# Three of eleven gate and up pairs of a gated FFN by seven block products, and the down product in two passes

## The chip, the cores and the metric

The kernel runs on one core of a Trainium2 chip. Its engines are TensorE (PE, with its weight load shown apart as PEld), VectorE (DVE), ScalarE (ACT), GpSimd (POOL) and SyncE (SP, which here only issues DMAs). The metric is the device time of one execution in microseconds; of several runs the median is given.

## The reference

One encoder block on 256 tokens of width 2048, all in float32. A mixer (a Hyena branch and a Conformer branch, gated and merged) comes first; behind it stands the channel part, which the change touches:

```python
h = rms_norm(x, ffn_pre_g[l])
gu = h @ ffn_w_gu[l]                               # 2048 x 11264
gate, up = gu[..., :FFN_HIDDEN], gu[..., FFN_HIDDEN:]   # FFN_HIDDEN = 5632
x = x + rms_norm((jax.nn.silu(gate) * up) @ ffn_w_down[l], ffn_post_g[l])
```

## The kernel before, in words

**Float32 in three products.** TensorE multiplies in a rounded float32 form (`F32R`), so each operand is split into a rounded part `hi` and the rest `lo`, and each product is hi·hi + lo·hi + hi·lo: three matmuls. For a weight tile of 128 partitions by 1024 elements (512 KB) the split is a cast on ScalarE (L299) and a subtraction on VectorE (L300), both in `split_raw`. The weight tile comes by a DMA from SyncE's queue into one of four `raw` buffers; `hi` and `lo` have three buffers each, so a tile's cast waits until TensorE has read the `hi` of the tile three before it.

**Gate and up.** `chunk_as` (L355) makes 512 columns of the result for all 256 tokens: eight groups, each of one weight tile (two contraction blocks of 128), and per group 2 blocks x 2 token halves x 3 = 12 matmuls of 128x128 by 128x512, 96 in a chunk. The activations are the stationary operand: `h2T`, eight tiles of 4 KB per partition, already split. The eleven pairs (a gate chunk, then an up chunk, L1133 to L1140) take two of the four PSUM banks called `main` per chunk. Then `silu` (ScalarE, L1116) and `glu` (VectorE, L817) turn a pair into 512 columns of the gated result; `glu` goes on to transpose it (eight transposes on TensorE, L1126, into the PSUM banks called `aux`), and splits it into two tiles of `hid` (a cast on ScalarE, L1128, and a subtraction on VectorE, L1129). All 22 `hid` tiles are there before the down product begins.

**Down.** `product_as` (L382) multiplies the 44 contraction blocks of `hid` with `w_down`. All 2048 columns and both token halves are summed at once, in four `aux` and four `main` banks. Each of the 88 weight tiles (one block, 1024 columns) feeds 12 matmuls. The last four blocks are held back, split into spare tiles, and run result by result (token half t, 512 columns n, 12 matmuls each), so that each of the eight results can be finished while the next runs. `done` in `post_norm` (L966) squares a result on ScalarE (L272), multiplies it by the gain on VectorE (`gained`), and at the last result of a token half makes the norm's factor (`late_rstd`) and calls `finish_block` (L1142), which adds the residual in five pieces on VectorE (L1148) and writes each out (L1151).

**Memory and order.** Everything that isn't a `raw`, `hi` or `lo` buffer, or one of eight 2 KB `t5` tiles, lies in one pool, `big`, of 35 slots of 4 KB per partition: `h2T` 8, `hid` 22, the residual 4, the gated results one each. Work that follows a chunk is written as a generator that yields estimated costs; `pump(budget)` after each group of matmuls steps the generators in the queue, which sets the program order. A list scheduler then orders each engine's instructions by that program order and by its own simulated times, and each engine runs its list strictly in order.

## Time and profile before

| | us |
|---|---|
| median of 3 runs (lowest, highest) | 1399.36 (1397.22, 1399.64) |
| the profiled execution, its own time | 1399.35 |
| its span, first to last instruction | 1397.5 |
| TensorE busy in the span | 1384.8 |
| VectorE busy | 867.2 |
| ScalarE busy | 669.2 |

The mean granted clock of TensorE was 0.997 of full speed. The busy time of TensorE is that of matmuls that overlap each other (one lasts 391 ns and the next begins 227 ns after it), so it hides gaps shorter than a matmul; the chain of waits, which counts the steps from one instruction to the next, is the finer measure. The time outside the span is 1.85 us.

### The profile page before, as it was taken

To read this page: it belongs to the slowest core of one execution; us is meant where nothing else is said; L and a number is where in the kernel's file an instruction comes from. 1 tells how busy PE (TensorE), PEld (TensorE's weight loads), DVE (VectorE), ACT (ScalarE), POOL (GpSimd) and SP (SyncE) were. 2 spreads that over 40 slices of the span, in tenths; PEclk is the share of its full clock that TensorE was granted. 3 is DMA by queue.
4 is the path that set the end of the run, shared out by engine and by line. 5 is a ranking of instruction groups with operands and counts; after the bars stand their busy time and mean duration, and the time that the engine had idled before them with its cause. 6 is when DMAs were issued, how large, how long until landed. Compare 5 with 4: busy or idle time off the path is not lost.

```text
span 1397.5 us, 16896 instructions
## 1 busy us (share of the span) xinstructions
PE 1384.8 (99%) x6438; PEld 1153.3 (83%) x6438; DVE 867.2 (62%) x1084; ACT 669.2 (48%) x844; POOL 11.9 (1%) x23
## 2 busy tenths in 40 slices
PE   9999999999999999999999999999999999999997
PEld 8888888888888878888888888888888888888885
DVE  6888777778777777547754544545455544444445
ACT  6556555455565444446744444444444444333343
POOL 0000000000000000000000000000000000000000
PEclk9999999999999999999999999999999999999999
DMA  9676555554454655755566666666666665656653
GB/s 343 214 218 200 152 184 178 166 166 151 150 190 145 185 161 160 274 191 183 182 194 184 194 192 186 193 185 193 190 187 190 187 220 190 193 195 194 197 185 132
DMA packets 76544, 264.58 MB, mean 189 GB/s; under 512 B 8689, under 2 KB 10002, under 8 KB 76464
## 3 DMA queue, kind: packets, MB, share of 16 engines
q1 hardware_dynamic: 75520, 261.74, 59.5%
q0 software_dynamic: 944, 1.77, 0.4%
q8 instruction: 50, 0.82, 0.2%
q14 instruction: 30, 0.25, 0.1%
HBM read 261.38 MB, written 2.10 MB: 189 GB/s over the span
## 4 chain that ended last, share of the span: by engine, by line
PE 98%; DVE 1%; DMA 0%; ACT 0%; SPq 0%; issue 0%; DVEq 0%; ACTq 0%
PE main L87 80%; PE aux L87 16%; PE aux L1126 1%; DMA raw<-in_w_in_dram 0%; PE aux L705 0%; PE aux L941 0%; PE aux L621 0%; PE aux L1020 0%; PE aux L578 0%; DVE big L1148 0%; DVE lo L300 0%; ACT t L272 0%; ACT hi L299 0%; SPq L156 0%; DVE t L201 0%
## 5 line engine op out<-in xcount | busy, mean ns | idle before, releaser
L300 DVE TENSOR_TENSOR lo<-raw,hi 128x1024 fp32r<-128x1024 f32 x447 | 546.2, 1223 | 435.5 <-ACT hi L299 408.8
L299 ACT CAST hi<-raw 128x1024 fp32r<-128x1024 f32 x447 | 470.7, 1054 | 634.2 <-PE main L87 593.2
L87 PE MATMUL main<-hi,big 128*128 128x512 f32 x2824 | 717.5, 391 | 1.8 <-ACT big L201 1.2
L87 PEld LDWEIGHTS main<-hi,big 128*128 128x128 f32 x2824 | 528.5, 188 | 112.3 <-ACT big L201 1.7
L87 PE MATMUL main<-lo,big 128*128 128x512 f32 x1412 | 392.0, 390 | 0.0
L87 PEld LDWEIGHTS main<-lo,big 128*128 128x128 f32 x1412 | 265.1, 188 | 55.3 <-issue 0.2
L87 PE MATMUL aux<-hi,big 128*128 128x512 f32 x416 | 111.7, 389 | 0.0
L87 PE MATMUL main<-big,hi 128*128 128x512 f32 (+1 forms) x448 | 97.8, 363 | 0.7 <-ACT hi L217 0.5
L87 PEld LDWEIGHTS aux<-hi,big 128*128 128x128 f32 x416 | 77.9, 188 | 16.1
L87 PEld LDWEIGHTS main<-big,hi 128*128 128x128 f32 x448 | 73.9, 190 | 13.4 <-ACT hi L217 1.5
L87 PE MATMUL aux<-big,big 128*128 128x512 f32 x288 | 76.5, 391 | 0.0
L87 PE MATMUL aux<-lo,big 128*128 128x512 f32 x208 | 64.3, 389 | 0.0
L87 PEld LDWEIGHTS aux<-big,big 128*128 128x128 f32 x288 | 53.7, 188 | 11.6 <-DVE big L300 0.4
L87 PEld LDWEIGHTS main<-big,lo 128*128 128x128 f32 x384 | 51.7, 191 | 3.1
L87 PE MATMUL main<-big,lo 128*128 128x256 f32 x384 | 53.2, 282 | 0.0
L87 PEld LDWEIGHTS aux<-lo,big 128*128 128x128 f32 x208 | 39.0, 188 | 8.1
L87 PE MATMUL main<-big,big 128*128 128x512 f32 x132 | 31.9, 393 | 0.0
L300 DVE TENSOR_TENSOR big<-raw,big 128x1024 fp32r<-128x1024 f32 x16 | 19.6, 1226 | 14.6 <-ACT big L299 14.5
L87 PEld LDWEIGHTS main<-big,big 128*128 128x128 f32 x132 | 24.4, 188 | 4.9
L299 ACT CAST big<-raw 128x1024 fp32r<-128x1024 f32 x16 | 16.8, 1053 | 18.1 <-DMA raw<-in_w_down_dram 9.5
L817 DVE SCALAR_TENSOR_TENSOR big<-main,rstd,big 128x512 f32<-128x512 f32 x22 | 15.5, 747 | 12.0 <-PE main L87 12.0
L663 ACT CAST big<-t 128x512 fp32r<-128x512 f32 x24 | 14.7, 618 | 6.4 <-DVE t L662 6.3
(212 smaller groups left out, 627.0 us busy)
## 6 DMA issues: line engine op xcount, KB each, us to landing
raw<-in_w_gu_dram SPq DMA_DIRECT2D x176, 512.0 KB
raw<-in_w_as_dram SPq DMA_DIRECT2D x96, 512.0 KB
raw<-in_w_down_dram SPq DMA_DIRECT2D x88, 512.0 KB
raw<-in_w_in_dram SPq DMA_DIRECT2D x44, 512.0 KB
raw<-in_w_out_dram SPq DMA_DIRECT2D x32, 512.0 KB
raw<-in_hy_proj_dram SPq DMA_DIRECT2D x16, 512.0 KB
raw<-in_cf_proj_dram SPq DMA_DIRECT2D x16, 512.0 KB
raw<-in_w_in_dram SPq DMA_DIRECT2D x8, 256.0 KB
```

The costliest lines, as they stand in the source:

```text
L87: return nc.tensor.matmul(o, lhsT, rhs, start=start, stop=stop, skip_group_check=True)
L299: S.copy(hi[:, k], raw[:, k])
L300: V.tensor_tensor(out=lo[:, k], in0=raw[:, k], in1=hi[:, k], op=ALU.subtract)
L663: nc.scalar.copy(rs[j][ft][:, 0], v)
L817: nc.vector.scalar_tensor_tensor(out=d[:, t], in0=ps[t], scalar=scale[t], in1=d[:, t], op0=ALU.mult, op1=ALU.mult)
L1126: nc.tensor.transpose(tr[:, c, t * P:(t + 1) * P], sg[:, t, f:f + P], ident)
```

## The change

Pairs 1, 2 and 3 of the eleven no longer go through `chunk_as`. The generator `seven` treats one pair as a product of 2 by 2 blocks: the tokens' two halves by the two halves of the 16 contraction blocks (`k`), times these halves by gate and up. It forms seven products of sums and differences of such blocks in place of eight products of blocks (Strassen's scheme in Winograd's form). The four sums of tokens are made once (`sums_of_tokens`) and split into eight slots; the four differences of weights are made for each pair on VectorE (`less`), from tiles that are loaded into `big` slots, and are then split as any weight tile. A pair takes twelve steps: in part one, four steps of two products (p1, p5); in part two, four of three (p3, p7, p6); in part three, four of two (p2, p4). A product has six matmuls in a step. Behind parts one, two and three the products are added up (`first_out`, `second_out`, `last_out`). After every second group of the other pairs' chunks, `tick` takes one step.

No result is turned into `hid` when it is made: the gated results stay as they are, one slot each, and `make_hid` transposes and splits each of them during the first pass of the down product. That product, `product_halves`, goes over all 44 blocks for the first 1024 columns and then again for the others, in four banks a pass; the results of the first pass are finished during the second, and the last four blocks of the second pass are held back.

```diff
+SEVENS = 3
...
     def chunk_as(w, act, budget):
...
             pump(budget)
+            tick()
         return ps
...
+    def product_halves(w, nkt, act, budget, late, done):
+        finished = deque()
+        for hf in range(2):
+            ps = [[(aux() if hf else psm.tile([P, 512], F32, tag="main", name=nm("main")))
+                   for _ in range(2)] for _ in range(2)]
+            held = []
+            for kt in range(nkt):
+                if not hf and kt % 4 == 0:
+                    hid = act(kt // 4)
+                ahead = hf and kt >= nkt - late
+                hi, lo = split_group(
...
+                if ahead:
+                    held.append((kt, hi, lo))
+                    continue
...
+                pump(budget)
+                if hf and kt and finished:
+                    done(*finished.popleft())
+            if not hf:
+                finished.extend((t, j, ps[t][j]) for t in range(2) for j in range(2))
...
+    def make_hid(c):
+        def begin(c):
+            if len(hid) == 2 * c and c < len(gated):
+                hid.extend(slot([P, 2, 2, T], F32R) for _ in range(2))
+                turning.append(push(to_hid(gated[c], hid[-2:]), front=not c))
+        begin(c)
+        drain(list(turning))
...
+        begin(c + 1)
+        return hid
...
+    def sums_of_tokens():
+        for m in range(4):
+            f, r = slot([P, 2, 2, T]), slot([P, 4, 2, P])
+            sh, sl = slot([P, 4, 2, P], F32R), slot([P, 4, 2, P], F32R)
...
+    def seven(i, v):
+        def load(q, m):
+            r = slot([P, 2, 512])
+            nc.sync.dma_start(r, a["w_st"][i, q, m])
+            return r
...
+        def product(o, of, m, parts):
+            hi, lo = parts
+            for j in range(2):
+                for n, (s, w) in enumerate(((0, hi), (1, hi), (0, lo))):
+                    mm(o, of(m, j, s), w[:, j, :], (m, j, n) == (0, 0, 0), (m, j, n) == (3, 1, 2))
...
+        def second_out(p6, p3, p7, u5, u1, u3, c12):
+            add(u3, p6, u1)
+            add(c12, u3, u5)
+            yield 1.4
+            add(c12, p3, c12)
+            add(u3, p7, u3)
+            yield 1.4
+            add(u5, u3, u5)
+            yield 0.7
...
+        for m in range(4):
+            b11, b12 = load(0, m), load(1, m)
+            w1 = split_raw(b11)
+            tt.append(slot([P, 2, 512]))
+            less(tt[m], b12, b11)
+            wt = split_raw(tt[m])
+            product(p1, token(0, 0), m, w1)
+            product(p5, total(1), m, wt)
+            yield
+        out = emptied(first_out(p5, p1, u5, u1))
+        for m in range(4):
+            b22, b12 = load(3, m), load(1, m)
+            w3 = split_raw(b22)
+            if m == 0:
+                drain(out)
+                p6, p3, p7 = aux(), aux(), aux()
+            product(p3, total(4), m, w3)
+            less(b12, b22, b12)
+            product(p7, total(3), m, split_raw(b12))
+            less(tt[m], b22, tt[m])
+            product(p6, total(2), m, split_raw(tt[m]))
+            yield
+        out = emptied(second_out(p6, p3, p7, u5, u1, u3, c12))
+        for m in range(4):
+            b21 = load(2, m)
...
+            product(p2, token(1, 0), m, split_raw(b21))
+            less(tt[m], b21, tt[m])
+            product(p4, token(1, 1), m, split_raw(tt[m]))
+            yield
+        ends.extend(emptied(last_out(p4, p2, u5, u1, u3, c12)))
...
+    def advance():
+        count[0] += 1
+        if count[0] % 2 == 0:
+            next(steps, None)
...
     for n in range(FFN // 512):
+        if 0 < n <= SEVENS:
+            continue
...
+        if n == 0:
+            push(sums_of_tokens())
+            ticks.append(advance)
...
-    post_norm(a["w_down"], FFN // P, hid, "ffn_post_g", "pd", 1.3, 8, finish_block)
+    post_norm(a["w_down"], FFN // P, make_hid, "ffn_post_g", "pd", 1.3, 4, finish_block,
+              product=product_halves)
```

## Rows read from the trace of the kernel before

**Rows 1.** The page's first part (busy microseconds, share of the span, instructions; PEld is TensorE's weight load) and its fourth (the chain of work that ended last, shares of the span by engine).

```profile
PE 1384.8 (99%) x6438; PEld 1153.3 (83%) x6438; DVE 867.2 (62%) x1084; ACT 669.2 (48%) x844; POOL 11.9 (1%) x23
...
PE 98%; DVE 1%; DMA 0%; ACT 0%; SPq 0%; issue 0%; DVEq 0%; ACTq 0%
```

**Rows 2.** The waits of TensorE's matmuls over the whole span: who waited for whom, microseconds in total, times, longest.

```profile
PE aux L87 <- POOL big L163: 1.3, 1, 1.3
...
PE main L87 <- ACT hi L299: 0.4, 2, 0.2
```

**Rows 3.** The chain of waits in order of time: start, microseconds, what. A piece from the filter stage, and from the gate and up stage one set of eight transposes and the pieces of two gate and up pairs (the 0.87 us left out between them are the next set of transposes).

```profile
106.09 31.66 PE main L87 x184
...
709.29 0.87 PE aux L1126 x8
710.16 43.55 PE main L87 x192
754.58 43.55 PE main L87 x192
```

**Rows 4.** Busy time by stage: the gate and up products after the first gate chunk, the down product without its last groups, those last groups, and what follows the last matmul. Columns: window, its length, busy time and count of PE, PEld, DVE, ACT and POOL, granted clock (1.00 is full speed), busy share of the DMA engines, GB/s.

```profile
687.23:1148.04 460.81, 460.81 (x2073) 382.52 (x2074) 231.46 (x214) 201.67 (x211) 0.00 (x0) 1.00 0.63 193
1148.04:1366.99 218.95, 218.95 (x971) 181.39 (x971) 102.03 (x86) 86.37 (x84) 0.00 (x0) 1.00 0.60 193
1366.99:1388.63 21.64, 21.60 (x94) 17.22 (x93) 13.90 (x25) 10.39 (x20) 0.00 (x0) 1.00 0.30 110
1388.63:1397.50 8.87, 0.00 (x0) 0.00 (x0) 4.22 (x10) 0.98 (x3) 0.00 (x0) 0.75 0.32 118
```

**Rows 5.** Groups of instructions by line and form: line, engine, operation, out<-in, shapes, count | busy time, mean nanoseconds of one | idle time of the engine before them and what ended it.

```profile
L300 DVE TENSOR_TENSOR lo<-raw,hi 128x1024 fp32r<-128x1024 f32 x447 | 546.2, 1223 | 435.5 <-ACT hi L299 408.8 <-PE main L87 20.8 <-issue 5.0
L299 ACT CAST hi<-raw 128x1024 fp32r<-128x1024 f32 x447 | 470.7, 1054 | 634.2 <-PE main L87 593.2 <-issue 16.1 <-DVE lo L300 7.1
L817 DVE SCALAR_TENSOR_TENSOR big<-main,rstd,big 128x512 f32<-128x512 f32 x22 | 15.5, 747 | 12.0 <-PE main L87 12.0
L1129 DVE TENSOR_TENSOR big<-aux,big 128x512 fp32r<-128x512 f32 x22 | 14.1, 682 | 0.0
L1128 ACT CAST big<-aux 128x512 fp32r<-128x512 f32 x22 | 11.8, 589 | 3.0 <-PE aux L1126 3.0
L379 DVE TENSOR_TENSOR big<-main,big 128x256 f32<-128x256 f32 x20 | 7.6, 416 | 0.3 <-ACT big L378 0.3
L598 ACT COPY t<-aux 128x512 f32<-128x512 f32 x8 | 4.7, 585 | 5.1 <-PE aux L87 5.1
```

**Rows 6.** VectorE in order of time, in the filter stage: start, microseconds, engine, line, operation.

```profile
88.00 1.22 DVE L300 TENSOR_TENSOR lo<-raw,hi 128x1024 fp32r<-128x1024 f32 x1
89.13 1.22 DVE L572 TENSOR_TENSOR big<-big,big 128x1024 f32<-128x1024 f32 x1
90.27 1.22 DVE L300 TENSOR_TENSOR lo<-raw,hi 128x1024 fp32r<-128x1024 f32 x1
91.40 0.68 DVE L573 TENSOR_TENSOR big<-big 128x512 f32<-128x512 f32 x1
92.00 1.28 DVE L565 TENSOR_TENSOR big<-aux,big 128x512 f32<-128x512 f32 x2
```

**Rows 7.** Busy time in a stretch of the filter stage, ahead of the gate and up stage (columns as in Rows 4).

```profile
88.00:132.00 44.00, 44.00 (x255) 38.74 (x254) 39.85 (x58) 25.96 (x35) 1.64 (x3) 1.00 0.66 196
```

**Rows 8.** One group of eight products' usual order in the gate and up stage, all engines in order of time.

```profile
892.23 1.07 PE L87 MATMUL main<-lo,big 128*128 128x512 f32 x4
892.43 1.05 ACT L299 CAST hi<-raw 128x1024 fp32r<-128x1024 f32 x1 [1.67 <-PE main L87]
893.13 1.98 PE L87 MATMUL main<-hi,big 128*128 128x512 f32 x8
893.51 1.23 DVE L300 TENSOR_TENSOR lo<-raw,hi 128x1024 fp32r<-128x1024 f32 x1 [1.49 <-ACT hi L299]
894.95 1.07 PE L87 MATMUL main<-lo,big 128*128 128x512 f32 x4
895.15 1.05 ACT L299 CAST hi<-raw 128x1024 fp32r<-128x1024 f32 x1 [1.67 <-PE main L87]
```

**Rows 9.** The page's sixth part: DMA issues on GpSimd's queue with KB each and microseconds from issue to landing; SyncE's issues come without a time.

```profile
big<-in_filt_dram POOLq DMA_DIRECT2D x1, 512.0 KB, 6.9
big<-in_fwd_dram POOLq DMA_DIRECT2D x1, 512.0 KB, 7.5
```

**Rows 10.** The change from the gate and up stage to the down stage, all engines in order of time.

```profile
1147.85 1.41 DVE L817 SCALAR_TENSOR_TENSOR big<-main,rstd,big 128x512 f32<-128x512 f32 x2 [1.09 <-PE main L87]
1147.87 1.07 PE L87 MATMUL aux<-hi,big 128*128 128x512 f32 x4
```

**Rows 11.** The end of the kernel, all engines in order of time, from the last square of the first 128 tokens on.

```profile
1377.75 0.60 ACT L272 ACTIVATE t<-aux 128x512 f32<-128x512 f32 x1 [1.83 <-PE aux L87]
...
1382.66 1.53 DVE L1148 SCALAR_TENSOR_TENSOR big<-big,pdr,big 128x512 f32<-128x512 f32 x3
...
1388.63 0.60 ACT L272 ACTIVATE t<-main 128x512 f32<-128x512 f32 x1 [2.03 <-PE main L87]
...
1389.35 0.29 ACT L201 ACTIVATE pd1y<-pdss,pd1h 128x1 f32<-128x1 f32 x1
...
1392.26 1.53 DVE L1148 SCALAR_TENSOR_TENSOR big<-big,pdr,big 128x512 f32<-128x512 f32 x3
```

More of the change, by code (lines that the diff above doesn't have):

```diff
@@ L353, in half_chunk, with tick @@
         return ps
+    ticks = []
+    def tick():
+        if ticks:
+            ticks[0]()
     def chunk_as(w, act, budget):
@@ L964, in piece, with post_norm @@
         return v[t][n // 2][:, (n % 2) * 512:(n % 2 + 1) * 512]
-    def post_norm(w, nkt, act, gname, tag, budget, late, finish, between=None):
+    def post_norm(w, nkt, act, gname, tag, budget, late, finish, between=None, product=product_as):
         pg = [slot([P, 1024]) for _ in range(2)]
@@ L994, in done @@
                 finish(t, og, rstd[:, t:t + 1], gained)
-        product_as(w, nkt, act, budget, late, done)
+        product(w, nkt, act, budget, late, done)
     xr = token_slots()
@@ L1108, in first_gate @@
         return ps
+    gated = [None] * (FFN // 512)
     hid = []
@@ L1117, in silu, with to_hid @@
         yield 0.1
-    def glu(ps, sg, dst):
-        yield from glu_by(ps, sg, (rstd2[:, 0:1], rstd2[:, 1:2]))
+    def to_hid(sg, dst):
         for i in range(2):
@@ L1130, in glu @@
             yield 0.7
+    turning = deque()
+    def make_hid(c):
[5 more added lines that the diff above has]
+        drain(list(turning))
+        turning.clear()
+        if c == len(gated) - 2:
+            drain(list(evac))
+            evac.clear()
+        begin(c + 1)
+        return hid
@@ new lines, in block_kernel @@
+    sums, ends = [], []
+    def sums_of_tokens():
+        for m in range(4):
+            f, r = slot([P, 2, 2, T]), slot([P, 4, 2, P])
+            sh, sl = slot([P, 4, 2, P], F32R), slot([P, 4, 2, P], F32R)
+            for j in range(2):
+                h = h2T[2 * m + j]
+                nc.vector.tensor_tensor(
+                    out=f[:, j], in0=h[:, :, 0, :], in1=h[:, :, 1, :], op=ALU.add)
+            yield 1.4
+            a11, a12, a21, a22 = (
+                f[:, :, k, t * P:(t + 1) * P] for t in range(2) for k in range(2))
+            for o, x, y, op in ((0, a21, a22, ALU.add), (1, r[:, 0], a11, ALU.subtract),
+                                (2, a11, a21, ALU.subtract), (3, a12, r[:, 1], ALU.subtract)):
+                nc.vector.tensor_tensor(out=r[:, o], in0=x, in1=y, op=op)
+            yield 1.7
+            nc.scalar.copy(sh, r)
+            nc.vector.tensor_tensor(out=sl, in0=r, in1=sh, op=ALU.subtract)
+            sums.append((sh, sl))
+            yield 1.2
@@ L1132, in block_kernel, with sevens @@
+    def sevens():
+        for i in range(SEVENS):
+            while len(sums) < 4 or "h_norm" not in done:
+                yield
+            gated[i + 1] = slot([P, 2, 512])
+            yield from seven(i, gated[i + 1])
+    steps = sevens()
+    count = [0]
+    def advance():
+        count[0] += 1
+        if count[0] % 2 == 0:
+            next(steps, None)
     w_gu = a["w_gu"]
     for n in range(FFN // 512):
+        if 0 < n <= SEVENS:
+            continue
         before_chunk()
-        sg = slot([P, 2, 512])
+        gated[n] = sg = slot([P, 2, 512])
@@ L1136, in block_kernel @@
         after_chunk(silu(first_gate(w_gu[0], 1.2) if n == 0 else chunk_as(w_gu[n], h2T, 1.2), sg))
+        if n == 0:
+            push(sums_of_tokens())
+            ticks.append(advance)
         before_chunk()
-        ps = chunk_as(w_gu[FFN // 512 + n], h2T, 1.2)
-        hid.extend(slot([P, 2, 2, T], F32R) for _ in range(2))
-        after_chunk(glu(ps, sg, hid[-2:]))
+        after_chunk(glu_by(
+            chunk_as(w_gu[FFN // 512 + n], h2T, 1.2), sg, (rstd2[:, 0:1], rstd2[:, 1:2])))
+    ticks.clear()
@@ L1142, in finish_block @@
+    for _ in steps:
+        pump(1.2)
+    drain(ends)
     def finish_block(t, og, rstd, last):
@@ L1218, in _layout, with quadrants @@
     w_in = np.asarray(i["w_in"][0])
+    def quadrants(w):
+        v = w.reshape(4, 2, 2, P, 2, FFN // 512, 512)[..., 1:1 + SEVENS, :]
+        v = v.transpose(5, 2, 4, 0, 3, 1, 6)
+        return v.reshape(SEVENS, 4, 4, P, 2, 512)
     x = np.asarray(i["x"][0])
@@ L1225, in _layout @@
         "cf_proj": tiled(np.asarray(i["cf_proj"][0]), 2, 512), "w_out": i["w_out"][0],
-        "w_gu": tiled(np.asarray(i["ffn_w_gu"][0]), 2, 512),
+        "w_st": quadrants(np.asarray(i["ffn_w_gu"][0])), "w_gu": tiled(np.asarray(i["ffn_w_gu"][0]), 2, 512),
         "w_down": i["ffn_w_down"][0], "w1": i["hy_filt_w1"][0], "w2": i["hy_filt_w2"][0],
```

49 lines of the change are left out of this document (added).

## The prediction

> **What bounds the kernel now.** I read the busy table and the shares of the chain of waits first [rows 1]: TensorE is busy 1384.8 of 1397.5 us and holds 98% of the chain. The list of TensorE's waits comes next [rows 2], because busy time hides gaps shorter than a matmul: the longest wait of the whole run is 1.3 us, at the start, and in all there are a few microseconds. Then the chain in order of time [rows 3]: each gate and up pair is one unbroken piece, 43.55 us for 192 matmuls, and the next pair starts 44.42 us later, the 0.87 us between being eight transposes. So a matmul costs 43.55 / 192 = 0.2268 us. Last the stages [rows 4]: over the gate and up stage VectorE is busy 231 of 461 us, ScalarE 202, the DMA engines 63%. TensorE alone sets the pace there and through the down product; a matmul taken out shortens the run by 0.2268 us, if nothing that is put in its place comes late.
>
> **What is removed.** A pair had 2 x 8 groups x 12 = 192 matmuls; seven products of 4 steps x 6 matmuls are 168. Three pairs: 72 matmuls less, 72 x 0.2268 = 16.33 us. All other matmuls stay: the down product has 88 tiles x 12 in either form, the 88 transposes only move from between the chunks into the first down pass. The new matmuls have the old shape (128x128 stationary, 512 columns), so the old step stands for them; nothing in the trace gives them another.
>
> On this the Trainium skill would give less: TensorE: Matmul & The Clock Gate, section Back-to-back issue gap, says that a sustained stream of weight loads and 512-column matmuls comes to some 131 ns per matmul. By that estimate the saving would be 72 x 0.131 = 9.4 us. The trace disagrees with 0.2268 us over 192 matmuls [rows 3], and the trace decides.
>
> **What is added on VectorE.** Durations in the groups are longer than the steps from start to start: in a full stretch, operations over 128x1024 that last 1.22 us start 1.13 us apart (88.00, 89.13, 90.27, 91.40), those over 128x512 0.60 us apart [rows 6]. A step of a pair by seven, with the two chunk groups beside it, holds: part one, 2 + 2 subtractions of splits and 1 difference, 5 x 1.13 = 5.7 us, beside 24 + 12 matmuls, 8.16 us; part two, 5 subtractions and 2 differences, 7.9 us beside 24 + 18 matmuls, 9.53 us; part three as part one. Over a pair: 4 x (5.7 + 7.9 + 5.7) = 77 us, and some 8 us for adding up the products (5 + 2 adds at 0.60) and for gating, the pair's own and that of the chunks beside it (L817, two in 1.41 us [rows 10]). That is 85 us beside 456 x 0.2268 = 103.4 us of TensorE: 82%, where VectorE now has 50% [rows 4]. That such a load alone stops nothing is seen in the filter stage: VectorE was busy 39.85 of 44 us [rows 7], and TensorE's chain ran on there for 31.66 us in one piece [rows 3].
>
> A stage average isn't enough, so I lay one step of part two on the clock, TensorE at 0: groups A to 2.72 and B to 5.44, then p3 to 6.80, p7 to 8.16, p6 to 9.53. A cast starts 0.2 us after the `hi` three tiles before it has been read (892.43 against the `lo` matmuls' start at 892.23) and takes 1.05, the subtraction follows 0.03 later with 1.23 [rows 8]. So p7's split is ready at 4.3 us, p6's at 7.1, the next A's at 9.1. Needed (`hi` at the first matmul, `lo` at the third of six, or the ninth of twelve) are p7's `lo` at 7.25, p6's at 8.6, A's at 11.3: slack 1.5 us or more everywhere. Between these subtractions VectorE has a gap of 1.6 us from 4.2 to 5.8 and two of 0.9, in which the two differences fit, one of them pushing a subtraction by 0.2. Part two in steady state then stalls nothing. Where a burst falls in (`second_out`: five adds, 3.0 us, against 2.5 us free in a step of part three) up to 0.5 us can come late, and `last_out` has 2.6. I take 0.5 us a pair, 1.5 us in all; below it the bound is 0 (TensorE's waits of this stage are under 0.5 us, so there is none to win), above it 9 us (the second rival). The sums of tokens: per block of four some 2 x 0.60 + 4 x 0.34 (L379's 0.416 [rows 5], less the 0.08 that neighbours overlap) + 1.13 us, 15 us in all, spread by the budget of 1.2 per group over some 16 groups (43.6 us) that hold 16 x 1.13 = 18 us: 77%, so covered; if the cover fails it is in the same 9 us. ScalarE casts 5 tiles in 9.53 us, 5.3 us busy [rows 5]; copies of products take 0.59 each (L598): covered.
>
> **What is added on DMA and in memory.** A pair loads 20 tiles for 16. In part one four loads of 0.524 MB fall in 8.16 us, 257 GB/s, where the stage now draws 193 GB/s at a share of 63% [rows 4]; scaled, that is 84%, no bound. By the code the `big` slots in use during the third pair's part two are 8 `h2T`, 8 sums, 4 residual, 9 gated, 4 `tt`: 33 of 35. So only one step's two loads fit, and the next ones wait on SyncE's queue, with the chunks' own loads behind them, until `b12` is split (4.3 us) and `b22` used. A load of 512 KB took 6.9 to 7.5 us from issue to landing on GpSimd's queue, the only ones with a time [rows 9]: landed at 11.8, difference, cast and subtraction 3.5 us later at 15.3, needed at 9.53 + 7.25 = 16.8. It fits by 1.5 us; I take nothing for it (bounds 0 and the last rival).
>
> **The handover to the down product.** Now the first down matmul follows the last gate and up matmul at once [rows 10]. After the change the first result must be transposed (0.87 us, paid already), copied (0.59, L1128) and its rest subtracted (0.68, L1129) before the second down matmul; VectorE is meanwhile on the last gating (1.41 us). Copy ready at 0.44 + 0.2 + 0.59 = 1.23, rest at some 2.3 us, TensorE free at 0.87 with one matmul to do between: 0.4 + 0.8 = 1.2 us idle. If the scheduler puts those transposes ahead of the last groups, 0; if a cast of 1.05 us stands in front, 2.5. I take 1.2 us. Between the passes nothing is late: the second uses the four `aux` banks, free by then, and the results of the first have 2.72 us each.
>
> **The end.** Now the last token half has 10.9 us of matmuls, in which VectorE's finish of the first half ends 1384.19 - 1377.71 = 6.5 us after that half's last matmul, and the root for the second starts 0.74 us after the last matmul (1389.35) [rows 11]. After it two results stand behind, 24 matmuls, 5.45 us. VectorE, in order, then has the gain of result 2 (0.60) and two small operations (0.3) to do at 6.5: the root can start at 7.4 in place of 5.45 + 0.74 = 6.2. So 1.2 us late (bounds 0, if the scheduler puts these ahead, and 2).
>
> **Sum**, against the profiled execution's own 1399.35 us (span 1397.5 and 1.85 around it; the median of the runs is 1399.36): 1399.35 - 16.33 + 1.5 + 1.2 + 1.2 = 1386.9 us.
>
> **The rivals.**
> - VectorE in program order. If the differences are not done early, VectorE waits for ScalarE's cast of each difference, 2 x 1.15 us in a step of part two: 7.9 + 2.3 = 10.2 against 9.53. Parts one and three stay under (6.8 of 8.16). 12 steps x 0.7 = 8.4 us in place of 1.5: 1393.8 us. For it: strict order on the engine, and VectorE's idle time is already spent on ScalarE's casts (408.8 of 435.5 us, L300 [rows 5]). Against: a difference needs no `hi` buffer and can fill VectorE's gaps.
> - The `lo` parts late. In a product of six, `lo` is wanted 0.45 us after `hi`, in a group of twelve 1.81. If each of the 48 products of differences waits 0.3 us for it, 14.4 us go and the run comes to 1383.0 + 2.4 + 14.4 = 1399.8: no change. Against: the 1.5 us of slack above.
> - Slower: loads held by slots. If a step's loads can't be issued before the step in front has let go of its tiles, a step lasts 7.5 + 3.5 + 0.3 = 11.3 us in place of 8.16 (part one) or 9.53 (part two): 3.1 or 1.8 us lost. In the eight such steps of the third pair that is 19.6 us: 1383.0 + 2.4 + 19.6 = 1405.0; with the second pair's too, 1424.6. It decides from 17 us lost. For it: 33 of 35 slots, and a queue that issues in order. Against: my count leaves five slots free in the second pair's part two, and a slack of 1.5 us in the third's.
>
> On the first rival the Trainium skill is harder: VectorE: DVE Perf Modes, section The DRAIN you can't avoid, has the next operation start only when the pipe of the one before is empty. The step would then be the duration, 1.22 us, part two 8.5 + 2.3 = 10.8 us, and that rival 1383.0 + 2.4 + 12 x 1.3 = 1401. The trace disagrees, with starts 1.13 us apart at durations of 1.22 [rows 6], so this takes nothing from the forecast's chance.
>
> **How the numbers follow.** Forecast 0.62 (1383 to 1391), VectorE in order 0.17, `lo` late 0.10, slots 0.11. What a measurement can't tell from no change is 0.2%, 2.8 us, so faster means under 1396.6, slower over 1402.2. The first two cases are faster, 0.79; the third is the same, 0.10; the fourth slower, 0.11. The range starts at 1382, the sum with every added cost at nothing (1383.0) less a microsecond of the runs' scatter, and ends at 1396.5, which takes in the VectorE rival with its handover and tail at their upper bounds.
>
> **What would show it.** TensorE with 6366 matmuls (72 fewer) at 0.227 us; over the stretch with the sevens VectorE busy about nine tenths in busy time and TensorE's waits for VectorE or ScalarE there at 1.5 us; a gap of 1.2 us on the chain at the start of the down product; the root of the second half 2 us after the last matmul, and a tail of about 10 us for 8.9. It is wrong if the chain passes through DMA or VectorE inside the stretch with the sevens for more than 5 us, or if the new matmuls step at another pace.

## The result, and the profile after

The kernel after took 1390.36 us (median of five runs, 1388.57 to 1393.90) against 1399.36: 9.0 us less, ratio 0.9941 [0.9931, 0.9952]. Forecast were 12.5 us less; the time lies at the upper end of the likeliest case's own range (1383 to 1391). The profiled execution took 1390.36 us, span 1388.5.

The page of the kernel after, its first and fourth parts (before: [rows 1]):

```profile
PE 1369.7 (99%) x6366; PEld 1138.2 (82%) x6366; DVE 984.3 (71%) x1217; ACT 709.1 (51%) x890; POOL 12.4 (1%) x23
...
PE 94%; DVE 3%; DMA 1%; ACT 1%; issue 0%; SPq 0%; DVEq 0%; ACTq 0%
```

TensorE has the 72 matmuls fewer that were forecast, VectorE 117 us of work more, and TensorE's share of the chain fell from 98 to 94%: something now comes late (the 1% of the DMA lies ahead of the pairs, at the mixer's output weights). TensorE's waits over the whole span say who is named, though a row counts only the standing still, not what follows it:

```profile
PE main L88 <- DVE lo L301: 3.2, 3, 1.8
PE main L88 <- ACT hi L300: 1.5, 4, 0.9
```

To find every loss I took the starts of all matmuls from the timeline of TensorE between the first up chunk (686.44) and the down product, and called lost what a step takes beyond 0.2268 us a matmul (0.109 a transpose). There are four places: 753 to 760 (3.66 us), 763 (1.07), 837 (0.98) and 882 (0.78), 6.5 us in all, every one in the first two of the three pairs. (Smaller losses, 0.28 us at 889.6 and a step longer by 0.11 us soon behind every stall, are left out here and bring the sum to 7.2 us more than in the kernel before.) The first of the four on the timeline, all engines (weight loads and copies left out):

```profile
752.07 2.35 DVE L1242 TENSOR_TENSOR big<-big,big 128x1024 f32<-128x1024 f32 x2
...
753.44 0.39 PE L88 MATMUL aux<-lo,big 128*128 128x512 f32 x1
753.64 1.04 ACT L300 CAST hi<-big 128x1024 fp32r<-128x1024 f32 x1 [1.66 <-PE aux L88]
754.34 1.22 DVE L301 TENSOR_TENSOR lo<-raw,hi 128x1024 fp32r<-128x1024 f32 x1
...
755.61 1.72 PE L88 MATMUL main<-lo,big 128*128 128x512 f32 x4 [1.78 <-DVE lo L301]
...
757.14 3.08 PE L88 MATMUL main<-hi,big 128*128 128x512 f32 x8
...
760.05 1.07 PE L88 MATMUL aux<-hi,big 128*128 128x512 f32 x4
```

VectorE does two differences (L1242), and the rest of a chunk's tile, which TensorE needs next, stands behind them and ends at 755.56. From 753.44 to 755.61 TensorE does one matmul: 2.17 - 0.23 = 1.94 us lost. The next twelve matmuls take 4.44 us (to 760.05) in place of 2.72: 1.72 us more, with no wait in it. Busy time by stretch (columns as in Rows 4):

```profile
700.00:1015.00 315.00, 310.86 (x1362) 255.50 (x1361) 255.69 (x239) 169.18 (x174) 0.00 (x0) 0.99 0.64 223
1378.65:1388.50 9.85, 0.00 (x0) 0.00 (x0) 6.08 (x16) 0.98 (x3) 0.00 (x0) 0.60 0.50 182
753.00:758.00 5.00, 3.21 (x11) 2.22 (x10) 5.00 (x6) 3.00 (x4) 0.00 (x0) 0.80 0.86 307
758.00:762.00 4.00, 4.00 (x16) 3.27 (x15) 4.00 (x4) 1.06 (x1) 0.00 (x0) 0.82 0.52 180
743.00:755.00 12.00, 10.83 (x48) 8.64 (x46) 11.88 (x11) 6.29 (x7) 0.00 (x0) 1.00 1.03 411
```

The granted clock is 0.80 and 0.82 in the stretches around and behind the stall: part of them ran at the lower of the two levels (1.2 GHz for 2.4). In finer stretches it is 1.00 from 754 to 756, 0.51 from 756 to 758, 0.64 from 758 to 760 and 1.00 again from 760 to 762, so it fell only behind the stall. The last row has VectorE busy for 11.88 of 12 us ahead of the stall, and the DMA engines full. What VectorE stood at before that is in its waits between 686 and 1040, and on its timeline:

```profile
DVE big L1242 <- DMA big<-in_w_st_dram: 7.8, 6, 2.7
```

```profile
714.77 1.23 DVE L1242 TENSOR_TENSOR big<-big,big 128x1024 f32<-128x1024 f32 x1 [2.07 <-DMA big<-in_w_st_dram]
...
742.77 1.23 DVE L1242 TENSOR_TENSOR big<-big,big 128x1024 f32<-128x1024 f32 x1 [2.68 <-DMA big<-in_w_st_dram]
...
834.68 1.23 DVE L1242 TENSOR_TENSOR big<-big,big 128x1024 f32<-128x1024 f32 x1 [2.08 <-DMA big<-in_w_st_dram]
```

Six times a difference stands for a tile that has not landed, for up to 2.68 us. Two of the long ones, 742.77 and 834.68, come 11 and 3 us before losses; behind the third, 714.77, nothing was lost. Why the tile was late is on SyncE's queue; its timeline, then its waits from 725 to 745:

```profile
728.76 0.90 SPq L1226 DMA_DIRECT2D big<-in_w_st_dram  x2
735.13 0.33 SPq L288 DMA_DIRECT2D raw<-in_w_gu_dram  x1
735.55 0.85 SPq L1226 DMA_DIRECT2D big<-in_w_st_dram  x2
...
737.78 3.96 SPq L1226 DMA_DIRECT2D big<-in_w_st_dram  x6
```

```profile
SPq L288 <- DVE lo L301: 14.6, 4, 6.6
```

Nothing is issued from 729.7 to 735.1: a chunk's load (L288) waits there for a `raw` buffer (the longest such wait, 6.6 us, ends just before, at 726.3), and the pair's loads (L1226) stand behind it in the order of the program. Then six go out in a burst, and VectorE gets its tile at 742.7.

The other two losses, at 763 and 882, have no such wait close ahead of them. At 763.20 a cast starts as TensorE lets go of a `hi` buffer, with one matmul left to do, and TensorE waits 0.91 us for it. Ahead of 882 the chain runs through VectorE alone, with a difference between two splits:

```profile
879.60 0.97 DVE lo L301
880.56 1.14 DVE big L1242
881.70 1.14 DVE lo L301
```

The two ends. The chain where the down product begins, and the timeline of ScalarE behind the last matmul (1378.65):

```profile
1134.19 5.47 PE main L88 x24
1139.67 0.87 PE aux L1173 x8
1140.54 1.60 PE main L88 x7
```

```profile
1378.68 0.60 ACT L273 ACTIVATE t<-aux 128x512 f32<-128x512 f32 x1 [2.03 <-PE aux L88]
...
1380.64 0.29 ACT L202 ACTIVATE pd1y<-pdss,pd1h 128x1 f32<-128x1 f32 x1 [1.27 <-DVE pd1h L202]
```

The down product begins with no idle time (1.2 us were forecast): the first result's eight transposes went among the matmuls before, and the second's eight follow 24 matmuls later. The root of the second token half starts 1.99 us after the last matmul, having waited for VectorE, and the tail is 9.85 us for 8.87 [rows 4].

### The profile page after: what moved, and what is told of

Its sections match the earlier page's. It is cut to its first block, busy times and chain, and to the rows that moved or that the text cites. A ratio compares the mean times of both kernels' runs of the same rounds, so it can differ in the third digit from the quotient of the medians.

```text
span 1388.5 us, 16998 instructions
## 1 busy us (share of the span) xinstructions
PE 1369.7 (99%) x6366; PEld 1138.2 (82%) x6366; DVE 984.3 (71%) x1217; ACT 709.1 (51%) x890; POOL 12.4 (1%) x23
## 4 chain that ended last, share of the span: by engine, by line
PE 94%; DVE 3%; DMA 1%; ACT 1%; issue 0%; SPq 0%; DVEq 0%; ACTq 0%
PE main L88 70%; PE aux L88 22%; DMA raw<-in_w_out_dram 1%; DVE lo L301 1%; PE aux L1173 1%; DVE big L202 0%; DMA raw<-in_w_in_dram 0%; DVE big L1355 0%; ACT hi L300 0%; PE aux L752 0%; PE aux L668 0%; PE aux L988 0%; DVE big L1242 0%; ACT big L300 0%; PE aux L625 0%
## 5 line engine op out<-in xcount | busy, mean ns | idle before, releaser
L301 DVE TENSOR_TENSOR lo<-raw,hi 128x1024 fp32r<-128x1024 f32 x403 | 491.4, 1222 | 289.9 <-ACT hi L300 255.2
L300 ACT CAST hi<-raw 128x1024 fp32r<-128x1024 f32 x403 | 423.6, 1053 | 522.1 <-PE main L88 378.4
L88 PE MATMUL main<-hi,big 128*128 128x512 f32 x2472 | 632.0, 391 | 2.9 <-ACT hi L300 1.3
L88 PEld LDWEIGHTS main<-hi,big 128*128 128x128 f32 x2472 | 462.4, 188 | 100.7 <-ACT hi L300 3.0
L88 PE MATMUL aux<-hi,big 128*128 128x512 f32 x752 | 213.5, 389 | 0.0
L88 PEld LDWEIGHTS aux<-hi,big 128*128 128x128 f32 x752 | 141.0, 188 | 29.1
L88 PE MATMUL aux<-lo,big 128*128 128x512 f32 x376 | 127.1, 389 | 0.0
L300 ACT CAST hi<-big 128x1024 fp32r<-128x1024 f32 x84 | 87.3, 1053 | 64.6 <-PE main L88 44.9
L301 DVE TENSOR_TENSOR lo<-big,hi 128x1024 fp32r<-128x1024 f32 x84 | 101.5, 1219 | 24.9 <-ACT hi L300 13.4
L1242 DVE TENSOR_TENSOR big<-big,big 128x1024 f32<-128x1024 f32 x48 | 57.9, 1219 | 7.9 <-DMA big<-in_w_st_dram 7.8
```

The lines of the kernel that those rows point to most:

```text
L88: return nc.tensor.matmul(o, lhsT, rhs, start=start, stop=stop, skip_group_check=True)
L300: S.copy(hi[:, k], raw[:, k])
L301: V.tensor_tensor(out=lo[:, k], in0=raw[:, k], in1=hi[:, k], op=ALU.subtract)
L1242: nc.vector.tensor_tensor(out=out, in0=x, in1=y, op=ALU.subtract)
```

## The experiments

Each was timed beside the kernel before on the same chip (median there 1398.4 to 1398.8 us), so the ratios are what is compared; the ratio of the kernel after is 0.994. "Lost" is TensorE's time as counted above. My theory after the first look: differences wait for loads that stand in SyncE's queue, and a VectorE that is 81% busy has no room to catch up. Rivals: VectorE's work alone; the price of the down product's new form; DMA traffic.

**The down product in two passes alone.** No pair by seven, no sums of tokens; `w_st` left out.

```diff
-SEVENS = 3
+SEVENS = 0
...
-            push(sums_of_tokens())
-            ticks.append(advance)
+            pass
```

> All eleven pairs go the old way; only the order of the second half is changed: the gated results stay, they are transposed in the first down pass, and the down product goes in two passes with four blocks held back. If the parts add up as the trace of the changed kernel reads (handover 0, end 1.0 us later, because the root of the second token half waits for VectorE's finish of the first), the run is 0.5 to 1.5 us longer than before, and the piece from the last matmul to the end is about 9.85 us for 8.87. The rival, that the two passes themselves cost what the forecast missed, expects 3 us or more above before.

1400.43 us, ratio 1.0009 [1.0000, 1.0018]: 1.6 us longer than before. Behind the last matmul, on ScalarE's timeline:

```profile
1387.30 0.60 ACT L273 ACTIVATE t<-aux 128x512 f32<-128x512 f32 x1 [2.03 <-PE aux L88]
...
1389.25 0.29 ACT L202 ACTIVATE pd1y<-pdss,pd1h 128x1 f32<-128x1 f32 x1 [1.26 <-DVE pd1h L202]
```

The root again comes 2 us after the last matmul, and the tail is 10.1 us for 8.9: 1.2 of the 1.6 us. At the handover 16 transposes and four matmuls fill the time until the first result is split, and some 0.6 us is lost. So the new form of the down product explains about a microsecond, not the 6.5.

**No differences.** The four `less` calls go and the tiles are split as loaded: the three pairs' results are other numbers. A step of part one so takes one `big` slot less, which the expectation doesn't count.

```diff
-            tt.append(slot([P, 2, 512]))
-            less(tt[m], b12, b11)
+            tt.append(b12)
...
-            less(b12, b22, b12)
...
-            less(tt[m], b22, tt[m])
...
-            less(tt[m], b21, tt[m])
```

> The kernel after, with the differences of weights left out: the loaded tiles are split and multiplied as they are (so the three pairs' results are other numbers), with the same loads, splits, matmuls and slots. If VectorE is what makes TensorE late, by its own load or by standing in order at a difference, the 6.5 us of TensorE's excess in the stretch with the sevens fall under 1.5 us, the granted clock there is 1.00 throughout, and the run comes to 1384 to 1386 us on the scale of before at 1399.4. If the loads are late for whoever needs them, the casts on ScalarE stand there instead and 3 us or more of the excess stay.

1383.66 us, ratio 0.9888 [0.9874, 0.9901]: 6.7 us less than the kernel after, and no step of TensorE there lost more than 0.35 us. Without the 48 differences the loss is gone. And it gained 15.2 us on the kernel before, with the tail's 1.0 us still in it: that fits the 16.3 of the forecast. By the estimate from the Trainium skill's 131 ns a matmul (TensorE: Matmul & The Clock Gate, section Back-to-back issue gap) it would have been 9.4 us at most, and this run doesn't agree with that. VectorE still waited for these loads, now in the split itself:

```profile
DVE lo L301 <- DMA big<-in_w_st_dram: 6.5, 5, 1.8
```

With VectorE busy 212 of 315 us (67%) that harmed nothing. This run alone can't say whether it was the work or the wait that hurt.

**Each step's loads one step earlier.** The same loads on the same queue; VectorE's work stays.

```diff
+    def take():
+        load_next()
+        return loaded.popleft()
...
-            b11, b12 = load(0, m), load(1, m)
+            b11, b12 = take()
...
+            if i == 0:
+                load_next()
                 yield
```

> The kernel after, with each step's weight loads issued one step earlier in program order, the first pair's first ones two groups before its first step. Theory one (VectorE stands at differences whose loads have not landed, 7.8 us in six waits, and the backlog behind makes TensorE late): those waits fall under 2 us, TensorE's excess in the stretch from 6.5 us to under 3, the run is 3 to 5 us shorter than the kernel after. Theory two (the differences are too much work for VectorE where they fall, loads or not): the excess stays at 5 us or more. Third possibility: with two more slots wanted in the third pair (37 of 35) the loads are held there and the third pair, which has no excess now, gets some.

1386.05 us, ratio 0.9905 [0.9890, 0.9920]. The stretch from 700 to 1015, a part of it, and VectorE's waits for these loads (its difference is L1253 here):

```profile
700.00:1015.00 315.00, 314.99 (x1392) 260.23 (x1390) 258.98 (x243) 172.03 (x176) 0.00 (x0) 1.00 0.65 226
743.00:755.00 12.00, 12.00 (x55) 9.94 (x54) 12.00 (x11) 5.51 (x6) 0.00 (x0) 1.00 0.90 315
```

```profile
DVE big L1253 <- DMA big<-in_w_st_dram: 5.6, 6, 1.7
```

TensorE is busy 314.99 of 315 us with VectorE at 82%, more than in the kernel after (81%). From 743 to 755 VectorE has no idle time at all, and TensorE loses nothing. So the load on VectorE that I forecast can be carried, and the DMA traffic too (226 GB/s for 223). The part that missed: I expected the waits for loads to go, and they fell only from 7.8 to 5.6 us, the longest from 2.7 to 1.7. So neither a full VectorE nor a wait for a tile stops TensorE by itself; in the kernel after the first loss came where a wait of 2.7 us was followed by 12 us of full work.

**Differences on GpSimd.**

```diff
-            nc.vector.tensor_tensor(out=out, in0=x, in1=y, op=ALU.subtract)
+            nc.gpsimd.tensor_tensor(out=out, in0=x, in1=y, op=ALU.subtract)
```

> The kernel after, with the 48 differences of weights made by GpSimd instead of VectorE. Nothing in the traces has such an operation on GpSimd over 128x1024. If it takes no more than about 3 us, both theories of VectorE's lateness expect the excess to fall under 2 us, and 1384 to 1387 us. If GpSimd is slower than 5 us each, part two (two differences in 9.5 us) is paced by it and the run is longer than the kernel after, above 1395 us; a slowing of VectorE's own operations beside GpSimd's would show in the mean of its subtractions (now 1222 ns).

1418.67 us, ratio 1.0136 [1.0123, 1.0150], slower than before. Groups by line and form:

```profile
L301 DVE TENSOR_TENSOR lo<-raw,hi 128x1024 fp32r<-128x1024 f32 x403 | 536.9, 1337 | 290.2 <-ACT hi L300 257.2 <-PE main L88 26.0 <-issue 5.3
L301 DVE TENSOR_TENSOR lo<-big,hi 128x1024 fp32r<-128x1024 f32 x84 | 151.5, 1825 | 20.0 <-ACT hi L300 12.0 <-PE main L88 7.0
L1242 POOL TENSOR_TENSOR big<-big,big 128x1024 f32<-128x1024 f32 x48 | 151.4, 3175 | 534.8 <-DMA big<-in_w_st_dram 455.6 <-DVE big L1268 35.6 <-DVE t L1245 34.3
```

A difference takes 3.18 us there for 1.22, and VectorE's subtractions beside it lengthen: 1337 ns for 1222 in the mean of all chunk tiles of the run, 1825 for 1219 in the pairs' own. The means mix two kinds. Splits that no GpSimd operation overlaps still take 1.22 us; from 748 to 771, where GpSimd subtracts without a break, two of them take 6.7 us:

```profile
748.20 23.35 POOL L1242 TENSOR_TENSOR big<-big,big 128x1024 f32<-128x1024 f32 x7
755.91 6.76 DVE L301 TENSOR_TENSOR lo<-raw,hi 128x1024 fp32r<-128x1024 f32 x2
```

The 3.18 us fall between the two cases of the expectation; the slowing of VectorE was named in it as a sign, without a price. The run doesn't tell the theories apart, as it gives VectorE other work and longer work.

**A step after every third group.** VectorE has less to do in the same time, and so has the DMA.

```diff
-        if count[0] % 2 == 0:
+        if count[0] % 3 == 0:
```

> The kernel after, with a step of a pair by seven after every third group of the chunks instead of every second: VectorE's work in part two is 9.1 us of 12.25 (74%) for 7.9 of 9.53 (83%), the loads are issued as before. The theory (a wait of VectorE for a load hurts because VectorE has no room behind it to catch up): waits for loads of the pair of some 5 to 9 us stay, TensorE's excess in the stretch falls from 6.5 us to under 2.5, and the run lies 2 to 5 us under the kernel after. Rival (the waits hurt by themselves, whatever room there is): an excess of 5 us or more. A few of the 36 steps come behind the last chunk, without groups beside them, and may cost about 1 us.

1414.24 us, ratio 1.0105 [1.0087, 1.0123]: slower than before, where I expected the loss to shrink. VectorE's waits for these loads grew fivefold though it is less busy (219 of 315 us); the timelines of SyncE and VectorE at the longest:

```profile
DVE big L1242 <- DMA big<-in_w_st_dram: 39.4, 14, 6.9
```

```profile
906.72 15.64 SPq L288 DMA_DIRECT2D raw<-in_w_gu_dram  x6
922.41 13.51 SPq L1226 DMA_DIRECT2D big<-in_w_st_dram  x7
```

```profile
928.62 1.22 DVE L1242 TENSOR_TENSOR big<-big,big 128x1024 f32<-128x1024 f32 x1 [6.62 <-DMA big<-in_w_st_dram]
```

Six chunk loads fill the queue for 15.6 us, at the pace at which `raw` buffers come free, and a step's loads begin to go out when VectorE already wants them. With more chunk loads between two steps the wait in the queue is longer. ScalarE stands for such a load too, and TensorE 2.7 us behind it, with VectorE idle for 8.75 us:

```profile
735.10 1.04 ACT L300 CAST hi<-big 128x1024 fp32r<-128x1024 f32 x1 [6.00 <-DMA big<-in_w_st_dram]
```

Here a late load alone makes TensorE late. In all TensorE loses about 28 us in the stretch, the lower clock behind its long stalls included. My theory had taken the waits as given and asked whether room on VectorE heals them; as the waits grew fivefold, the run doesn't answer that, but it puts the queue's order first.

**The pair's loads on GpSimd's queue**, with a step after every second group and after every third.

```diff
-            nc.sync.dma_start(r, a["w_st"][i, q, m])
+            nc.gpsimd.dma_start(r, a["w_st"][i, q, m])
```

> The kernel after, its 60 loads of the three pairs' weights issued from GpSimd's queue instead of SyncE's; nothing else is changed. Theory (the loads are late because they stand, in order, behind chunk loads that wait 6 to 9 us for a raw buffer): VectorE's waits for these loads fall from 7.8 us to under 2, TensorE's excess in the stretch from 6.5 us to under 2, and the run is 4 to 6 us shorter than the kernel after, 1384 to 1386.5 us. Rival (too few slots, or the DMA engines' rate, holds the loads): the waits stay at 5 us or more. Rival (VectorE's load as such): waits go, the excess stays.

> A step after every third group, as in the run at 1414 us, with the loads on GpSimd's queue. If the order of SyncE's queue made that run slow (39 us of VectorE's waits for loads, 14 of them), they fall under 4 us and the run comes under 1389 us, about 25 us less than with SyncE's queue; VectorE at 74% in part two then leaves no excess in the stretch over 2 us. If the scheduler's spreading of the steps itself was the cause, it stays above 1405 us.

1387.77 us, ratio 0.9921 [0.9908, 0.9935], and 1391.67 us, ratio 0.9953 [0.9940, 0.9967]: 2.6 us less than the kernel after and 22.6 us less than the same schedule on SyncE's queue. VectorE's waits for these loads: none in the first, and in the second

```profile
DVE big L1242 <- DMA big<-in_w_st_dram: 3.0, 3, 1.3
```

in place of 39.4. Bytes and VectorE's work are the same, so the waits went with the place in the queue. (The scheduler also set the engines' instructions in a somewhat other order than with SyncE's queue; what that is worth wasn't tried apart.) The Trainium skill (DMA: Bandwidth & Descriptors, section Rules for kernel authors) says that spreading DMAs over issuing engines doesn't help bandwidth and only saves issue time. Here it also took loads out from behind one that waits for a buffer, in a change that was worth 22.6 us. Both runs missed their expectation by some microseconds, and both still lost time with hardly a wait for a load. The first lost 3 us, in two places, close to the 763 and the 882 of the kernel after, like this (ScalarE's timeline, then TensorE's):

```profile
763.41 1.04 ACT L300 CAST hi<-big 128x1024 fp32r<-128x1024 f32 x1 [2.08 <-PE aux L88]
```

```profile
763.21 0.40 PE L88 MATMUL aux<-lo,big 128*128 128x512 f32 x1
764.51 0.74 PE L88 MATMUL aux<-hi,big 128*128 128x512 f32 x2 [0.90 <-ACT hi L300]
```

A cast can begin only when TensorE has let go of a `hi` buffer, and TensorE has one matmul left by then.

The second lost about 9 us, where I had expected 2 at most: 4.6 of them from 791 to 800, and 2.9 from 1130 to 1135, where the down product begins. At the first place ScalarE stands, in its order, at the `silu` of a chunk that TensorE hasn't finished, and VectorE waits for a cast behind that (the granted clock is 0.68 from 795 to 800):

```profile
788.66 1.27 ACT L1164 ACTIVATE big<-main,rstd 128x512 f32<-128x512 f32 x2 [4.61 <-PE main L88]
790.90 1.22 DVE L301 TENSOR_TENSOR lo<-big,hi 128x1024 fp32r<-128x1024 f32 x1 [4.45 <-ACT hi L300]
```

Three differences and the casts that need them come in a row after that, while TensorE waits. So the queue explains most of these 39.4 us of waits and of the loss behind them, but not every loss: the order on the two engines and the number of `hi` buffers cost too.

**Four `hi` and four `lo` buffers as well**, paid for with two slots of `big`.

```diff
-    big = ctx.enter_context(tc.tile_pool(name="big", bufs=35))
+    big = ctx.enter_context(tc.tile_pool(name="big", bufs=33))
...
-            hi = wp.tile([P, 2, 512], F32R, tag="hi", name=nm("hi"))
-            lo = wp.tile([P, 2, 512], F32R, tag="lo", name=nm("lo"))
+            hi = wp.tile([P, 2, 512], F32R, tag="hi", name=nm("hi"), bufs=4)
+            lo = wp.tile([P, 2, 512], F32R, tag="lo", name=nm("lo"), bufs=4)
```

> The loads on GpSimd's queue, four hi and four lo buffers in place of three, and 33 big slots in place of 35 to pay for them. In the run with the queue alone some 2.9 us of TensorE's excess were left in the stretch, at two places, where a cast starts only when TensorE has read the hi of the product right in front (763.4, 884). If three hi buffers are what is short, both places go and the excess falls under 1 us: the run 1.5 to 3 us shorter than with the queue alone, 1385 to 1386.5 us, unless the two slots less cost something ahead of the stretch. If it is VectorE's order, 2 us or more stay.

1380.77 us, ratio 0.9871 [0.9858, 0.9883]: the best of all, 17.8 us under the kernel before on that chip. In the stretch TensorE lost 0.6 us (VectorE's and TensorE's waits, 686 to 1200):

```profile
DVE big L1242 <- DMA big<-in_w_st_dram: 5.6, 6, 2.4
```

```profile
PE aux L88 <- ACT hi L300: 0.5, 1, 0.5
```

VectorE again waits for loads, once for 2.4 us, and with splits made one tile further ahead TensorE doesn't feel it. It is more than was expected: of 6.3 us between this span and that of the run with three buffers, 3.3 are gained ahead of the pairs: by the starts of matmuls 2.1 between 516 and 525, where the chain there passes through VectorE and ScalarE, and 0.8 at 640, behind three waits of 4 to 6 us for the mixer's output weights. Another 2.6 lie between the first up chunk and the down product. Whether the buffers or the smaller pool did the first wasn't tried apart, nor were four buffers with the loads left on SyncE's queue.

**Eight blocks held back in the second pass, and the sums later.** Three runs, on top of the loads a step ahead (the first two) and of the GpSimd queue (the third).

```diff
-    post_norm(a["w_down"], FFN // P, make_hid, "ffn_post_g", "pd", 1.3, 4, finish_block,
+    post_norm(a["w_down"], FFN // P, make_hid, "ffn_post_g", "pd", 1.3, 8, finish_block,
```

> The loads a step ahead, and eight blocks of the second down pass held back instead of four, so that the first token half has 10.9 us of matmuls behind it again. If the end is late because VectorE is still at the first half's finish when the second half's last result is there, the root comes 0.74 us after the last matmul for 1.98, the piece behind the last matmul is 8.6 to 9.1 us for 9.85, and the run is about 1 us shorter than with the loads alone. If the second half's lateness has another cause, the piece stays at 9.6 us or more.

> As the one before, and the sums of tokens put behind the first up chunk in program order. In the kernel after, operations of the sums stand on the chain between 668 and 672 us, where the second token half is being normed, and the piece from the mixer's last product to the first up chunk is 43.26 us for 42.34 before. If the sums cause that, it comes to 42.3 to 42.6 us, and the run is 0.5 to 1 us shorter than the one before it (which five rounds may not tell apart); if not, it stays at 43 us or more.

> The loads on GpSimd's queue and eight blocks held in the second down pass. The end of 8.6 us behind the last matmul (for 9.85) should come on top of the queue's gain: 1 us less than with the queue alone, 1383 to 1385.5 us, beside 1383.3 with the loads a step ahead.

1383.27 us, ratio 0.9891 [0.9876, 0.9906]; 1383.83 us, ratio 0.9897 [0.9882, 0.9912]; 1386.98 us, ratio 0.9920 [0.9906, 0.9933]. In the first the root follows the last square at once (ScalarE's timeline):

```profile
1372.35 0.60 ACT L273 ACTIVATE t<-aux 128x512 f32<-128x512 f32 x1 [4.75 <-PE aux L88]
...
1373.07 0.29 ACT L202 ACTIVATE pd1y<-pdss,pd1h 128x1 f32<-128x1 f32 x1
```

0.72 us after the start of that square, for 1.96 in the kernel after: behind the last half's longer run VectorE is done with the other half in time. The tail is 8.6 us, 1.3 less. The run is 2.8 us faster than the one with loads a step ahead, but that one's runs lay between 1382.84 and 1386.42 and the profiled spans (1380.9 and 1381.1) hardly differ, so no more than the tail's 1.3 us is shown. In the second the sums of tokens are made behind the first up chunk: from the mixer's last product (its piece of 32 matmuls) to the first up chunk it takes 42.36 us, as in the kernel before (42.34), for 43.26 in the kernel after. Of these 0.9 us about half is the sums': a break of TensorE at 673 that every kernel with the sums in their old place has. The other half comes and goes: the run with the two passes alone takes 42.82 us without any sums, and the one with the loads on GpSimd's queue 42.81 with them. With the sums moved the stretch loses 1.6 us for 1.0: nothing is won. The third missed its 1383 to 1385.5 us: it has the shorter tail (8.9 us for 10.1), but its time is only 0.8 us under the same queue with four blocks, which their runs don't tell apart.

**The kernel after once more**, unchanged.

> The kernel after, unchanged, beside the one above on the same chip, as the scale for the comparisons: 1389 to 1392 us. TensorE's excess in the stretch with the sevens, 6.5 us in the first profile, should come again at the same places (the third step of the first pair's part two, the second pair's part one and two) if the order of the queues makes it, and move if it is chance.

1390.34 us (six runs, 1388.81 to 1392.67), ratio 0.9943 [0.9932, 0.9955]. It lost 1.54, 1.06, 0.85 and 0.77 us at the same four places, 4.2 us in all: the stalls belong to the schedule. Only the slow matmuls behind the first are missing; the granted clock there was 1.00.

## Why the prediction was right in its direction and 3.5 us short

- **What is removed: right.** 72 matmuls fewer, and the new ones step at 0.2268 us where nothing is late. The run of loads a step ahead shows it as a whole: from the first up chunk to the last matmul it takes 15.9 us less than the kernel before, with some 0.6 us of gaps.
- **Stalls among the pairs: the term that was mis-sized.** Forecast 1.5 us (0 to 9), measured 6.5 at four places and 7.2 over all matmuls, of which some 1.7 is the lower clock behind one stall. The steps that failed are three. On the clock of one step I laid casts, differences and splits, but took the tiles as there. For the loads I counted slots and bytes ("it fits by 1.5 us; I take nothing for it"), not what stands ahead of them on the queue. And the "slack 1.5 us or more everywhere" held for the order I had laid out, not for every order that the scheduler makes. Late loads stand before two of the four places (4.6 of the 6.5 us); loads a step ahead and the own queue take these two away, and more chunk loads between the steps make the loss larger. The other two (1.9 us) have no late load close before them, and places like them remain with the own queue. One more `hi` and `lo` buffer, beside that queue, leaves 0.6 us of loss, with waits for loads of up to 2.4 us. VectorE's share alone isn't the cause: 82% of it ran without a loss.
- **A sign of being wrong came true.** I had named more than 5 us of the chain through VectorE inside the stretch; it is 9.3 us (750.9 to 755.6, 835.8 to 838.4, 879.6 to 882.8). So the mechanism of the forecast, that nothing put in comes late, didn't hold, though the time lies in the range.
- **The rival "VectorE in program order"** (1393.8; its 8.4 us are what the bound of 9 stands for, not the second rival) came near in size. Its share was forecast about rightly (81% against 82; the nine tenths among the signs were too high, as the view counts overlapped time once). Its own mechanism, a wait for the cast of each difference in every step of part two, isn't what the four places show, and the same load ran without a loss; at 882 the order on VectorE does cost, 0.8 us. In its harder form (1401) I left out that the section I drew on, in the Trainium skill (VectorE: DVE Perf Modes, section The DRAIN you can't avoid), also says that an operation that isn't held starts earlier; the starts 1.13 us apart [rows 6] don't contradict it.
- **`lo` late**: TensorE does wait for `lo`, 3.2 us in three waits, two of them behind late loads and one behind VectorE's order; elsewhere it came in time.
- **The slower rival** named the queue that issues in order, but put its price on slots in the third pair. That pair, where slots are scarcest, lost nothing; the first two did, in part behind a wait for a `raw` buffer.
- **Handover: 1.2 forecast, 0 measured.** The case that I gave as the lower bound came about: the scheduler put the transposes ahead. With the two passes alone it was about 0.6, and with a step after every third group on GpSimd's queue 2.9.
- **The tail: right**, by its mechanism too: 1.0 us for 1.2, the root 1.99 us after the last matmul for about 2, and holding eight blocks takes it away.
- **The sums of tokens: taken as covered, cost about 0.5 us**, as the scheduler put them into the norming of the second token half, where VectorE is on the chain.

The sum by measured terms, on the profiled spans. From the first up chunk (687.23 and 686.44) to the end of the last matmul (1388.59 and 1378.65) it is 9.15 us less: 16.3 for the matmuls, less the 7.2 that were lost. The tail takes 1.0 more, and the first up chunk begins 0.8 earlier: 8.95 less, as measured (9.0). The 0.8 isn't a gain of the change: that start lay between 685.5 and 688.1 in the profiles of the kernels that leave the code ahead of it as it was. The stalls cost 5.7 us more than forecast, the handover 1.2 and the tail 0.2 less, and this start came 0.8 sooner: together the 3.5. That the time fell within 1383 to 1391 is so in part luck, and the room above it had been left for VectorE's order, not for late loads. Also open: why three `hi` buffers lost 3 us with the own queue and almost nothing with loads a step ahead, and what the two together would give with four buffers; the pool has too few slots for that, and it wasn't tried.

## What to carry to other kernels

When a change adds loads, look at the queue that issues them before counting bytes: a load is late by what the one in front of it waits for, and a loop's loads wait for buffers by design. Give a new stream its own queue, or issue it one step earlier. And lay the real order of the engines on the clock, not only a regular step: with an engine that works in order at four fifths of its time, one buffer more behind it can be what keeps TensorE fed. (That was tried only together with the own queue.)

## What the hardware showed that I had not expected

- Behind a stall of 1.78 us the granted clock was 0.51 (756 to 758) and 0.64 (758 to 760), and the twelve matmuls there took 1.72 us more. In the second profile of the same kernel the same place lost 1.5 us and the clock stayed at 1.00.
- GpSimd's two-input subtraction of 128x1024 in float32 takes 3.18 us in the mean, and VectorE's splits beside it slow: to 3.4 us for 1.22 where GpSimd works without a break. Three VectorE operations that read one input from PSUM and lay wholly beside a GpSimd one took 0.68 to 0.74 us, as without it. The Trainium skill (GPSIMD Engine Reference, section Key points) has the two engines contend for SBUF when VectorE reads two inputs there; the run agrees.
- The 60 loads of 512 KB took 4.9 us (median) from issue to landing on GpSimd's queue, for 6.9 and 7.5 of the two in the kernel before [rows 9].
